# SwiGLU in Strassen's 2x2 blocks with gate/up and down as two stages, and a one-pass output projection

## The chip, the cores and the metric

The kernel runs on 1 core of one Trainium2 chip. The time is the device time of one execution in microseconds (us); lower is better. The engines are TensorE (PE, with its weight loads as PEld), VectorE (DVE), ScalarE (ACT), GpSimd (POOL) and SyncE (SP), whose queue issues the DMAs here. SBUF and PSUM are the memories on the core (matmuls write PSUM); a DRAM tile lies outside the core.

## The reference

Two layers on x of 1024 rows (S) by 1024 columns (D), all in float32; layer 0 mixes tokens by sliding-window attention (A), layer 1 by stick-breaking attention (B), and each is followed by a SwiGLU of width 2816:

```python
def swiglu(h, w_gate, w_up, w_down):
    return (jax.nn.silu(h @ w_gate) * (h @ w_up)) @ w_down

cond = jax.nn.silu(c)
for i in range(2):
    mod = (cond @ ada_w[i] + ada_b[i])[:, None, :]
    sh1, sc1, g1, sh2, sc2, g2 = jnp.split(mod, 6, axis=-1)
    h = rmsnorm(x, norm1_g[i]) * (1.0 + sc1) + sh1
    y = attention_A_or_B(h)            # ends with o @ w_o
    x = x + g1 * y
    h = rmsnorm(x, norm2_g[i]) * (1.0 + sc2) + sh2
    x = x + g2 * swiglu(h, w_gate[i], w_up[i], w_down[i])
```

## The kernel before

Every float32 product is made of three matmuls (`mm3`): each operand is split into a high part, which ScalarE casts to float32r, and a low part, which VectorE gets by subtracting the high from the whole (`split_w`, `sub`); the matmuls are high x high, high x low, low x high, each 128 rows by 128 columns of stationary weights with 512 moving columns. A weight tile `wr` of 128x1024 is loaded by SP, split into `wh` and `wl`, and used.

After the attention of a layer has written its heads' outputs to DRAM (`odA`, `odB`), `out_proj` multiplies them by the output weights in two passes of 512 columns (`c` = 0 and 1). For each of eight blocks of 128 rows it reloads the block (`or`), casts it on ScalarE (`oh`), subtracts on GpSimd (`ol`), and runs 24 matmuls; VectorE adds the result to x (`xt`), which stays in SBUF. The first pass is spread over the attention's end by the scheduler, which orders instructions by their dependences and the code. After blocks 0 to 3 and 4 to 7 of the second pass, `norm_half` normalizes the rows, turns them by TensorE and splits them (`hth`, `htl`).

`swiglu` then goes over 11 pairs of 128-column slices: for a pair it computes gate and up for both slices (banks `psd` and `psz`), Silu on ScalarE and the product on VectorE (`sg`), splits it (`hh`, `hl`), and, one pair behind, the down product of the pair before for all 16 blocks of output, which VectorE adds from PSUM (`pst`, `psa`) to `xt`:

```python
        for c in range(NC):
            hid = [gate_up(2 * c), gate_up(2 * c + 1)]
            ada_some(ada_per)
            ...
            if prev is not None:
                down(c - 1, prev, False)
            prev = hid
```

`ada_some` puts conditioning work between: each step loads a 128x1024 tile of `ada_w` (`ada`), and VectorE accumulates it (`acc`, L257). In layer 0 there are five a pair, in layer 1 none. The gate row of the conditioning (`grow`) multiplies the down weights on VectorE (L319). GpSimd has no work in `swiglu`. Layer 0's results go to DRAM tiles `xsp` for the second mixer, layer 1's to the output, block by block as the last pair ends.

## Time and profile before

| | |
|---|---|
| median of 3 runs | 2609.93 us (2608.35 to 2610.12) |
| span of the profiled execution | 2603.6 us |
| TensorE busy | 2508.4 us (96%), 11932 matmul records |
| VectorE busy | 1501.7 us (58%) |
| ScalarE busy | 930.9 us (36%) |
| GpSimd busy | 256.8 us (10%) |
| mean granted TensorE clock | 0.989 |

The span runs from the first to the last instruction of the execution that was profiled; the time of an execution also holds what lies around it, so the median is 6.3 us above the span. Busy time of an engine says how long it worked, not that something waited for it.

### The profile page before, as it was taken

What the parts mean: (1) busy time and instruction counts of PE and PEld (TensorE: products, weight loads), DVE (VectorE), ACT (ScalarE), POOL (GpSimd) and SP (SyncE); (2) the same over time, 40 slices, a digit from 0 to 9 for tenths busy, and PEclk for the clock granted to TensorE, in tenths of its full rate; (3) what the DMA queues carried; (4) which work ended last, traced back from release to release, by engine and by line L of the source; (5) the groups of instructions that cost most, each with busy time, mean ns of one, the idle gap of its engine ahead of it and who ended that gap; (6) DMA issues with size and microseconds to landing.
All of it is one profiled execution on the core that took longest, in us unless ns stands there. A gap on an engine that the chain in (4) does not pass through costs nothing.

```text
span 2603.6 us, 30732 instructions
## 1 busy us (share of the span) xinstructions
PE 2508.4 (96%) x11932; PEld 2021.0 (78%) x11932; DVE 1501.7 (58%) x2229; ACT 930.9 (36%) x1789; POOL 256.8 (10%) x385
## 2 busy tenths in 40 slices
PE   5799889999999999999999999999999999999999
PEld 5677677888888888777777777767788888888887
DVE  6689866535435445456777887786533333333334
ACT  4487733211111111135566666564421111111110
POOL 2445551000000000010000000003300000000000
PEclk9899999999999999999999999999999999999999
DMA  8113683413323323121110001134321111111101
GB/s 269 57 36 102 184 204 92 122 57 105 92 71 105 89 74 102 51 97 34 33 32 25 25 23 32 31 110 109 78 65 49 49 49 49 49 49 49 49 17 65
DMA packets 199409, 194.03 MB, mean 75 GB/s; under 512 B 8144, under 2 KB 169056, under 8 KB 199264
## 3 DMA queue, kind: packets, MB, share of 16 engines
q1 hardware_dynamic: 198640, 191.92, 25.6%
q8 instruction: 94, 1.54, 0.2%
q14 instruction: 51, 0.42, 0.1%
q10 hardware_dynamic: 624, 0.14, 0.0%
HBM read 175.26 MB, written 16.78 MB: 74 GB/s over the span
## 4 chain that ended last, share of the span: by engine, by line
PE 77%; DVE 10%; ACT 5%; DMA 4%; POOL 3%; issue 3%; SPq 0%; ACTq 0%; POOLq 0%; DVEq 0%
PE psd L97 29%; PE psz L97 22%; PE pst L97 14%; PE psa L97 9%; PE pst L105 2%; DMA ada<-in_ada_w_dram 2%; DVE acc L257 1%; DVE wl L302 1%; DVE nb L818 1%; ACT sm L523 1%; DVE al L108 1%; ACT ah L835 1%; POOL ol L302 1%; DVE bb L820 1%; DMA wr<-in_w_down_dram 0%
## 5 line engine op out<-in xcount | busy, mean ns | idle before, releaser
L97 PE MATMUL psd<-hth,wh 128*128 128x512 f32 x1088 | 431.3, 396 | 1.1 <-ACT nt L345 1.1
L97 PE MATMUL psd<-hth,wl 128*128 128x512 f32 x1088 | 430.6, 396 | 0.0
L97 PE MATMUL psd<-htl,wh 128*128 128x512 f32 x1088 | 428.8, 394 | 0.0
L97 PE MATMUL psz<-htl,wh 128*128 128x512 f32 x704 | 274.3, 390 | 0.0
L97 PE MATMUL psz<-hth,wh 128*128 128x512 f32 x704 | 274.3, 390 | 0.0
L97 PE MATMUL psz<-hth,wl 128*128 128x512 f32 x704 | 274.0, 389 | 0.0
L302 DVE TENSOR_TENSOR wl<-wr,wh 128x1024 fp32r<-128x1024 f32 x122 | 152.5, 1251 | 181.8 <-ACT wh L301 180.3
L301 ACT CAST wh<-wr 128x1024 fp32r<-128x1024 f32 x122 | 128.5, 1056 | 349.2 <-PE psd L97 174.0
L97 PEld LDWEIGHTS psd<-hth,wh 128*128 128x128 f32 x1088 | 204.6, 188 | 45.0 <-issue 5.0
L97 PEld LDWEIGHTS psd<-hth,wl 128*128 128x128 f32 x1088 | 204.6, 188 | 41.8 <-issue 3.4
L685 DVE TENSOR_TENSOR xt<-pst,xt 128x512 f32<-128x512 f32 x242 | 165.2, 689 | 124.3 <-PE pst L97 124.2
L97 PEld LDWEIGHTS psd<-htl,wh 128*128 128x128 f32 x1088 | 204.7, 188 | 40.1 <-issue 2.3
L668 DVE TENSOR_TENSOR sg<-psz,sg 128x512 f32<-128x512 f32 x88 | 60.6, 688 | 276.0 <-PE psz L97 276.0
L97 PE MATMUL pst<-dh,hh 128*128 128x512 f32 x484 | 189.9, 393 | 2.8 <-DVE xt L685 2.3
L97 PE MATMUL pst<-dl,hh 128*128 128x512 f32 x484 | 189.6, 392 | 0.8 <-DVE dl L302 0.8
L97 PE MATMUL pst<-dh,hl 128*128 128x512 f32 x484 | 189.0, 391 | 0.0
L301 ACT CAST dh<-wr 128x1024 fp32r<-128x1024 f32 x44 | 44.9, 1052 | 387.3 <-PE pst L97 379.4
L818 DVE TENSOR_TENSOR_SCAN nb<-nb,ones 128x128 f32<-128x128 f32 (+7 forms) x128 | 169.5, 1342 | 4.4 <-ACT nb L813 4.3
L670 ACT CAST hh<-sg 128x512 fp32r<-128x512 f32 x88 | 54.6, 621 | 286.1 <-DVE sg L668 286.1
L97 PEld LDWEIGHTS psz<-hth,wl 128*128 128x128 f32 x704 | 132.2, 188 | 27.8 <-issue 0.2
L97 PEld LDWEIGHTS psz<-htl,wh 128*128 128x128 f32 x704 | 132.0, 187 | 27.8 <-issue 0.5
L97 PEld LDWEIGHTS psz<-hth,wh 128*128 128x128 f32 x704 | 132.2, 188 | 27.5 <-issue 0.2
(258 smaller groups left out, 4699.5 us busy)
## 6 DMA issues: line engine op xcount, KB each, us to landing
ada<-in_ada_w_dram SPq DMA_DIRECT2D x96, 512.0 KB, 4.4
wr<-in_w_gate_dram SPq DMA_DIRECT2D x44, 512.0 KB, 4.0
wr<-in_w_up_dram SPq DMA_DIRECT2D x44, 512.0 KB, 4.9
wr<-in_w_down_dram SPq DMA_DIRECT2D x44, 512.0 KB, 3.7
wr<-in_wqkv_b_dram SPq DMA_DIRECT2D x24, 512.0 KB, 3.9
or<-odA SPq DMA_DIRECT2D x32, 256.0 KB, 4.6
or<-odB SPq DMA_DIRECT2D x32, 256.0 KB, 4.5
wr<-in_wqkv_a_dram SPq DMA_DIRECT2D x10, 512.0 KB, 5.8
```

Of the source, the lines that this page charges most:

```text
L97: nc.tensor.matmul(o, l, r, start=start, stop=stop)
L105: nc.tensor.transpose(o, i, ident[:n, :n])
L108: return nc.vector.tensor_tensor(o, a, h.bitcast(F32), op=ALU.subtract)
L257: i = nc.vector.scalar_tensor_tensor(a, wt, condT[:, j : j + 1], a, op0=ALU.mult, op1=ALU.add)
L301: nc.scalar.copy(h, raw)
L302: (eng or nc.vector).tensor_tensor(l, raw, h.bitcast(F32), op=ALU.subtract)
L523: nc.scalar.activation(sm[:, h], sm[:, h], AF.Exp, bias=nm_[:, h : h + 1], scale=r[:, h : h + 1], accum_out=su[:, h : h + 1])
L668: nc.vector.tensor_tensor(sg, pu, sg, op=ALU.mult)
L670: nc.scalar.copy(hh[:, c0 : c0 + 512], sg)
L685: nc.vector.tensor_tensor(xs, pb, xs, op=ALU.add)
L818: nc.vector.tensor_tensor_scan(rv, rv, ones[:, 0:1].to_broadcast([P, L]), initial=1.0, op0=ALU.mult, op1=ALU.mult)
L820: nc.vector.tensor_tensor(bb[:, 0 : L - 1], bb[:, 0 : L - 1], nb[:, 1:L], op=ALU.mult)
```

## The change

*Output projection.* `out_proj` now loads the whole rows of the output weights, splits them, and runs both column halves of a block together, so each block is loaded and split once instead of twice. The sums go to `xsp` in DRAM as well. The norm keeps the same steps, but its results are the four quarters of the turned activations: B11 and B21 from rows 0 to 511 (columns 0 to 511 and 512 to 1023 of D), B12 and B22 from the other rows. VectorE makes from them T1 = B12 - B11, T2 = B22 - T1, T3 = B22 - B12 and N4 = B21 - T2, and seven operands (B11, B21, T1, T2, T3, N4, B22) are split and kept.

*SwiGLU.* The products are made by Strassen's scheme (the form of Winograd), seven products of blocks for eight. `gates` goes over 11 chunks of 256 columns: GpSimd forms four sums of each weight's quarters, each operand is split (`sh`, `sl`, six tiles each), and each of seven products of each weight is 12 matmuls; VectorE adds PSUM results to the first product `p1`. The gate values of a chunk are written to a DRAM tile `hid`. Only when all chunks are done, `down` starts: the accumulators `xa` are loaded from `xsp`, and pairs of `hid` and down weights in three rounds of 4, 4 and 3 chunks. In each round GpSimd forms eight sums per chunk and adds 12 results to the accumulators, VectorE multiplies the weights by the gate row and splits, and TensorE runs 7 products of 12 matmuls per chunk. `ada_some` uses the three buffers `wr` of the new pool `wf` in layer 0.

```diff
+    def out_proj(wo, od, x_src, x_dst, row, side_h, side_w, l, gi):
...
+        wcur[:] = [wf, "wr", 3]
...
+        def block(b):
+            raw = op.tile([P, KT, P], F32, tag="or", name=nm("or"), bufs=1)
+            for par in range(2):
+                nc.sync.dma_start(raw[par * HD : (par + 1) * HD], od(b, par))
+            oh, ol = split_w(raw, [P, KT, P], op, "oh", "ol", bufs=2, eng=nc.gpsimd)
...
+            for c in range(2):
+                cs_ = slice(c * 512, c * 512 + 512)
+                pb = bank_any()
+                for k in range(KT):
+                    wh, wl = W[k // 2]
+                    mm3(pb, oh[:, k], ol[:, k], wh[:, k % 2, cs_], wl[:, k % 2, cs_], k == 0, k == KT - 1)
+                nc.vector.tensor_tensor(xt[:, cs_], pb, xt[:, cs_], op=ALU.add)
+            nc.sync.dma_start(x_dst[b], xt)
...
+        def put(n, kk, t):
+            h, l_ = H[n]
+            nc.scalar.copy(h[:, kk], t)
+            sub(l_[:, kk], t, h[:, kk])
...
         for b in range(NB):
-            block(b, 0, W, lambda: bank("d"))
+            block(b)
             ada_some(1)
+            if b == 3:
...
+                rows(range(4))
+                for k in range(KT):
+                    put("B11" if k < 4 else "B21", k % 4, col(range(4), k))
...
+        rows(range(4, 8))
+        for kk in range(4):
+            b12 = col(range(4, 8), kk)
+            b22 = col(range(4, 8), kk + 4)
+            t1 = np_.tile([P, 512], F32, tag="nt", name=nm("nt"), bufs=4)
+            h11, l11 = H["B11"]
+            h21, l21 = H["B21"]
+            tt(t1, b12, h11[:, kk].bitcast(F32), op=ALU.subtract)
+            tt(t1, t1, l11[:, kk].bitcast(F32), op=ALU.subtract)
+            tt(b12, b22, b12, op=ALU.subtract)
+            put("B22", kk, b22)
+            tt(b22, b22, t1, op=ALU.subtract)
+            put("T2", kk, b22)
+            put("T3", kk, b12)
+            put("T1", kk, t1)
+            tt(t1, h21[:, kk].bitcast(F32), b22, op=ALU.subtract)
+            tt(t1, t1, l21[:, kk].bitcast(F32), op=ALU.add)
+            put("N4", kk, t1)
...
+    def split_s(wf, src, shape):
+        h = wf.tile([P, 512], F32R, tag="sh", name=nm("sh"), bufs=6)
+        l = wf.tile([P, 512], F32R, tag="sl", name=nm("sl"), bufs=6)
...
+        nc.scalar.copy(hv, src)
+        nc.vector.tensor_tensor(lv, src, hv.bitcast(F32), op=ALU.subtract)
+        return h, l
...
+        def chunk(c):
+            m = []
+            for w in (w_gate[l], w_up[l]):
+                raw = wf.tile([P, KT, 2 * P], F32, tag="wr", name=nm("wr"), bufs=3)
...
+            for x in m:
+                A = x["A"]
+                pt_(A[1, 0], A[1, 0], A[1, 1], op=ALU.add)
+                pt_(A[0, 0], A[1, 0], A[0, 0], op=ALU.subtract)
+                pt_(A[0, 1], A[0, 1], A[0, 0], op=ALU.subtract)
+                x["Y"] = bank("z")
+                mms(x, x["Y"], A[0, 0], "T2", True)
+                x["u2"] = tile_()
+                tt(x["u2"], x["Y"], x["p1"], op=ALU.add)
...
+            for x in m:
+                mms(x, x["Z"], x["A"][0, 1], "B22", False)
+                tt(x["u2"], x["Z"], x["u2"], op=ALU.add)
+            for n, i, j in (("p1", 1, 0), ("u3", 1, 1), ("u2", 0, 1)):
+                g = m[0][n]
+                nc.scalar.activation(g, g, AF.Silu)
+                tt(g, m[1][n], g, op=ALU.mult)
+                nc.sync.dma_start(hid[c][:, i, j * 512 : j * 512 + 512], g)
...
+    ROUNDS = (4, 4, 3)
...
+                for nm_, src in (("A", hid[c]), ("B", w_down[l][2 * c * P : 2 * (c + 1) * P].rearrange("(k p) n -> p k n", p=P))):
...
+                    nc.sync.dma_start(raw, src)
+                    if nm_ == "B":
+                        tt(raw, raw, row[:, None, :].to_broadcast([P, 2, D]), op=ALU.mult)
...
+            def prod(banks, a, b, start, before=None):
+                for j, x in enumerate(pairs):
+                    if before:
+                        before(x)
+                    ah, al = split_s(wf, a(x), [P, 512])
+                    bh, bl = split_s(wf, b(x), [P, 512])
+                    for t in range(4):
+                        s_ = slice(t * P, (t + 1) * P)
+                        mm3(banks[t], ah[:, s_], al[:, s_], bh, bl, start and j == 0, j == n - 1, not start)
...
+                pt_(xacc[t + 4][:, lo], xacc[t + 4][:, lo], p, op=ALU.add)
...
+            def s1(x):
+                pt_(x["tA"], x["A"][:, 0, hi], x["A"][:, 1, hi], op=ALU.add)
+                pt_(x["tB"], x["B"][:, 0, hi], x["B"][:, 0, lo], op=ALU.subtract)
...
+            def s4(x):
+                pt_(x["A"][:, 0, lo], x["A"][:, 0, lo], x["A"][:, 0, hi], op=ALU.subtract)
+                pt_(x["B"][:, 0, hi], x["B"][:, 1, hi], x["B"][:, 0, hi], op=ALU.subtract)
+
+            prod(X, lambda x: x["A"][:, 0, lo], lambda x: x["B"][:, 0, hi], False, s4)
+            for t in range(4):
+                u = p2.tile([P, 512], F32, tag="u", name=nm("u"), bufs=3)
+                tt(u, X[t], p1[t], op=ALU.add)
+                pt_(xacc[t + 4][:, hi], xacc[t + 4][:, hi], u, op=ALU.add)
```

Four places of the new order of instructions, each engine's own. TensorE at the end of layer 0's attention, before (VA and DV are the attention's values, `KTs` its keys, `qs` its queries; `oh` and `ol` the projection's block, `wh` and `wl` its weights):

```order
L97 MATMUL psd_3828<-wh_3801,ol_3823 128x512
L97 MATMUL psa_3463<-ph_3459,VA 128x512
L97 MATMUL psz_3428<-KTs,QT_3392 128x256 x4
L97 MATMUL psd_3828<-wh_3808,oh_3822 128x512
L97 MATMUL psa_3463<-pl_3460,VA 128x512
L97 MATMUL psa_3463<-ow_3466,DV 128x512
L493 MATMUL pst_3559<-identr,qs_3552 128x128
L97 MATMUL psa_3463<-ow_3469,DV 128x512
```

and now:

```order
L97 MATMUL psa_3762<-ph_3758,VA 128x512
L97 MATMUL psa_3762<-pl_3759,VA 128x512
L97 MATMUL psa_3762<-ow_3765,DV 128x512
L97 MATMUL psa_3762<-ow_3768,DV 128x512
L97 MATMUL psd_3858<-Wh_816_3820,oh_3852 128x512
L97 MATMUL psd_3858<-Wl_817_3821,oh_3852 128x512
L97 MATMUL psd_3858<-Wh_816_3820,ol_3853 128x512
```

The projection's matmuls stood among the attention's; now the first one stands behind the last of the attention.

VectorE at the end of layer 0's norm, before (the casts and subtractions of the last three slices):

```order
L108 TENSOR_TENSOR htl_949_4543<-nt_4609,hth_948_4542 128x512
L346 CAST hth_948_4542<-nt_4618 128x512
L108 TENSOR_TENSOR htl_949_4543<-nt_4618,hth_948_4542 128x512
L346 CAST hth_948_4542<-nt_4627 128x512
L108 TENSOR_TENSOR htl_949_4543<-nt_4627,hth_948_4542 128x512
L346 CAST hth_948_4542<-nt_4636 128x512
```

and now (`nt` are the turned slices and the sums made of them, `hB`, `hT` and `hN` the casts, `lB`, `lT` and `lN` the low parts; `sl` the low parts of weights; the end of the last of four such pairs of slices and the rows behind it):

```order
L108 TENSOR_TENSOR lN_920_4489<-nt_4594,hN_919_4488 128x512
L679 TENSOR_TENSOR nt_4625<-nt_4625,lB_828_3846 128x512
L680 TENSOR_TENSOR nt_4616<-nt_4623,nt_4616 128x512
L682 TENSOR_TENSOR nt_4623<-nt_4623,nt_4625 128x512
L108 TENSOR_TENSOR lT_922_4491<-nt_4625,hT_921_4490 128x512
L108 TENSOR_TENSOR lT_918_4487<-nt_4616,hT_917_4486 128x512
L108 TENSOR_TENSOR lT_916_4485<-nt_4623,hT_915_4484 128x512
L686 TENSOR_TENSOR nt_4625<-hB_829_3847,nt_4623 128x512
L687 TENSOR_TENSOR nt_4625<-nt_4625,lB_830_3848 128x512
L108 TENSOR_TENSOR lN_920_4489<-nt_4625,hN_919_4488 128x512
L703 TENSOR_TENSOR sl_4734<-wr_4647,sh_4733 128x512
L703 TENSOR_TENSOR sl_4756<-wr_4650,sh_4755 128x512
```

Where a cast and a subtraction stood for each slice, there are 11 operations for each pair of slices, and the third product's weights (`sl_4734` and `sl_4756`, of T2) follow after the last of them.

VectorE at the step from chunk 3 to chunk 4 of layer 0's gates, now (`f` are gate values, `acc` the conditioning's accumulation; there is no such place before):

```order
L257 TENSOR_SCALAR acc_5832<-ada_5830,condT 128x1024
L279 SCALAR_TENSOR_TENSOR gscT<-adaT,cols 128x8
L260 SCALAR_TENSOR_TENSOR acc_5832<-ada_5834,condT,acc_5832 128x1024
L764 TENSOR_TENSOR f_5664<-pst_5754,f_5664 128x512
L260 SCALAR_TENSOR_TENSOR acc_5832<-ada_5837,condT,acc_5832 128x1024
L768 TENSOR_TENSOR f_5642<-f_5664,f_5642 128x512
L260 SCALAR_TENSOR_TENSOR acc_5832<-ada_5840,condT,acc_5832 128x1024
L703 TENSOR_TENSOR sl_5851<-wr_5843,sh_5850 128x512
```

The first split of chunk 4's gate weight, `sl_5851`, stands behind the last additions of chunk 3 (`f_5664`, `f_5642`) and three accumulations.

SP at the end of layer 0's gates. Before, it issued here the last down weights and the first of the second mixer:

```order
L317 DMA wr_8904<-in_w_down_dram 128x1024
L317 DMA wr_8911<-in_w_down_dram 128x1024
L251 DMA ada_9046<-in_ada_w_dram 128x1024
L317 DMA wr_9063<-in_w_down_dram 128x1024
L317 DMA wr_9070<-in_w_down_dram 128x1024
L312 DMA wr_9437<-in_wqkv_b_dram 128x8x128
```

and now (`hid` are writes of gate values, `xa` accumulators, `rx` a pair's two halves):

```order
L769 DMA hid_3786<-f_7659 128x512
L769 DMA hid_3786<-f_7777 128x512
L888 DMA xa_7951<-xsp_3787 128x1024
L769 DMA hid_3786<-f_7737 128x512
L888 DMA xa_7953<-xsp_3788 128x1024
L888 DMA xa_7955<-xsp_3789 128x1024
L888 DMA xa_7957<-xsp_3790 128x1024
L888 DMA xa_7959<-xsp_3791 128x1024
L888 DMA xa_7961<-xsp_3792 128x1024
L888 DMA xa_7963<-xsp_3793 128x1024
L888 DMA xa_7965<-xsp_3794 128x1024
L795 DMA rx_7974<-hid_3777 128x2048
```

Between the last two writes of gate values and the pairs' loads, the loads of seven accumulators were put; the other pairs' loads follow `rx_7974`.

## Rows read from the trace of the kernel before

**Rows 1.** the page: span, busy time, chain by engine
```profile
span 2603.6 us, 30732 instructions
...
PE 2508.4 (96%) x11932; PEld 2021.0 (78%) x11932; DVE 1501.7 (58%) x2229; ACT 930.9 (36%) x1789; POOL 256.8 (10%) x385
...
PE 77%; DVE 10%; ACT 5%; DMA 4%; POOL 3%; issue 3%; SPq 0%; ACTq 0%; POOLq 0%; DVEq 0%
...
```

**Rows 2.** the chain that ended last, 478 to 490: start, us, what
```profile
...
480.69 5.44 PE psd L97 x24
...
```

**Rows 3.** windows: length, busy us of PE, PEld, DVE, ACT, POOL, PEclk, DMA, GB/s
```profile
...
290.00:337.00 47.00, 44.08 (x223) 34.45 (x222) 40.74 (x83) 30.20 (x80) 25.78 (x21) 1.00 0.77 224
...
357.00:425.00 68.00, 59.94 (x282) 49.73 (x281) 42.83 (x52) 29.69 (x41) 28.37 (x24) 0.95 0.59 146
425.00:1090.00 665.00, 661.39 (x2950) 546.37 (x2949) 315.43 (x383) 116.33 (x150) 0.00 (x0) 1.00 0.29 88
...
1828.00:1878.00 50.00, 46.06 (x233) 38.43 (x232) 22.00 (x34) 21.85 (x32) 21.51 (x22) 1.00 0.37 74
1878.00:2603.00 725.00, 720.45 (x3171) 594.50 (x3170) 286.62 (x364) 122.75 (x160) 0.00 (x0) 1.00 0.16 48
...
```

**Rows 4.** windows of the tile oh's matmuls, 280 to 340 and 1740 to 1790
```profile
...
sum 60.00, PE 26.42; mean PE 4.40
...
sum 50.00, PE 12.15; mean PE 2.43
```

**Rows 5.** the page, DMA issues: count, KB each, median us to landing
```profile
...
or<-odA SPq DMA_DIRECT2D x32, 256.0 KB, 4.6
...
```

**Rows 6.** groups by line and form: count, busy us, mean ns, idle before
```profile
...
L257 DVE SCALAR_TENSOR_TENSOR acc<-ada,condT,acc 128x1024 f32<-128x1024 f32 x77 | 101.2, 1315 | 76.6 <-DMA ada<-in_ada_w_dram 76.3
...
L302 POOL TENSOR_TENSOR ol<-or,oh 128x1024 fp32r<-128x1024 f32 x32 | 81.7, 2553 | 104.3 <-ACT oh L301 95.7 <-PE psd L97 7.8 <-DMA xt<-in_x_dram 0.8
...
L301 ACT CAST oh<-or 128x1024 fp32r<-128x1024 f32 x32 | 33.6, 1051 | 48.0 <-PE psd L97 35.9 <-PE pst L97 3.3 <-PE psz L97 3.3
...
L484 POOL TENSOR_TENSOR qs<-qn,qs 128x512 fp32r<-128x512 f32 x16 | 21.6, 1356 | 13.2 <-ACT qs L483 13.2
...
```

**Rows 7.** the timeline of VectorE and of TensorE, 415 to 422
```profile
...
415.49 0.68 DVE L622 TENSOR_TENSOR xt<-psa,xt 128x512 f32<-128x512 f32 x1
...
420.92 0.69 DVE L108 TENSOR_TENSOR htl<-nt,hth 128x512 fp32r<-128x512 f32 x1
421.52 0.42 DVE L346 CAST hth<-nt 128x512 fp32r<-128x512 f32 x1
...
419.22 0.33 PE L105 MATMUL psd<-ident,xn 128*128 128x128 f32 x1 [0.96 <-DVE xn L336]
...
```

**Rows 8.** windows of 5 and 20 us near loads
```profile
...
15.00:20.00 5.00, 4.14 (x20) 3.71 (x19) 4.21 (x5) 2.52 (x4) 1.57 (x3) 1.00 1.02 413
20.00:25.00 5.00, 0.00 (x0) 0.00 (x0) 4.86 (x5) 0.00 (x0) 0.00 (x0) 0.73 1.09 338
380.00:400.00 20.00, 15.80 (x75) 13.61 (x74) 13.40 (x19) 8.85 (x13) 6.68 (x7) 0.83 0.79 221
...
```

**Rows 9.** the timeline of GpSimd and of VectorE, 342 to 352
```profile
...
342.80 2.39 POOL L302 TENSOR_TENSOR ol<-or,oh 128x1024 fp32r<-128x1024 f32 x1 [6.64 <-ACT oh L301]
349.51 3.08 POOL L302 TENSOR_TENSOR ol<-or,oh 128x1024 fp32r<-128x1024 f32 x1 [4.33 <-ACT oh L301]
...
343.60 3.80 DVE L597 TENSOR_TENSOR wr<-wr,grow 128x1024 f32<-128x1024 f32 x2 [1.05 <-DMA wr<-in_wo_a_dram]
...
349.13 1.22 DVE L302 TENSOR_TENSOR xl<-wr,xh 128x1024 fp32r<-128x1024 f32 x1
```

**Rows 10.** the timeline of GpSimd and of VectorE, 308 to 312
```profile
...
308.84 2.39 POOL L302 TENSOR_TENSOR ol<-or,oh 128x1024 fp32r<-128x1024 f32 x1 [0.81 <-DMA xt<-in_x_dram]
...
310.26 0.67 DVE L108 TENSOR_TENSOR pl<-pst,ph 128x512 fp32r<-128x512 f32 x1
...
```

**Rows 11.** the timeline of SP's queue, its first loads
```profile
...
7.90 10.42 SPq L251 DMA_DIRECT2D ada<-in_ada_w_dram  x6
...
```

More of the change, by code (lines that the diff above doesn't have):

```diff
@@ new lines, in block, with rows @@
+            nc.sync.dma_start(x_dst[b], xt)
+            xts[b] = xt
+        def rows(bs):
+            for b in bs:
+                junk = np_.tile([P, D], BF16, tag="junk", name=nm("junk"), bufs=1)
+                ss = cons.tile([P, 1], F32, tag="ss", name=nm("ss"), bufs=3)
+                nc.scalar.activation(junk, xts[b], AF.Square, scale=1.0 / 32.0, accum_out=ss)
+                nc.gpsimd.tensor_scalar(ss, ss, EPS, None, op0=ALU.add)
+                nc.gpsimd.tensor_tensor(ss, ss, mhalf[:, 0:1], op=ALU.pow)
+                nc.vector.tensor_scalar(xts[b], xts[b], ss, None, op0=ALU.mult)
@@ new lines, in out_proj @@
+            if b == 3:
+                if l == 0:
+                    while ada_list:
+                        ada_some(1)
+                    gsc_make(0, 1)
+                rows(range(4))
+                for k in range(KT):
+                    put("B11" if k < 4 else "B21", k % 4, col(range(4), k))
+        pools.close(cm_o)
+        pools.close(cm_W)
+        cm_h2, h2 = pools.open(nm("h2"), side_w)
+        for n in ("T2", "T3", "N4", "T1", "B22"):
+            H[n] = (h2.tile(Q4, F32R, name=nm("h" + n)), h2.tile(Q4, F32R, name=nm("l" + n)))
@@ new lines, in mixer @@
+    def mixer(l, wo, od, x_src, row, side_h, side_w, gi, ada_per, rest, finish):
+        H, wf, cm_f, cm_h1, cm_h2 = out_proj(wo, od, x_src, xsp, row, side_h, side_w, l, gi)
+        if l == 0:
+            ada_list.extend(ada_late)
+        cm_fp, fp = pools.open(nm("fp"), side_h)
+        row2 = gates(l, H, wf, fp, hid, ada_per)
+        rest()
+        pools.close(cm_fp)
+        pools.close(cm_h1)
+        pools.close(cm_h2)
+        cm_xa, xa = pools.open(nm("xa"), "right")
+        cm_p2, p2 = pools.open(nm("p2"), "left")
+        xacc = []
+        for b in range(NB):
+            t = xa.tile([P, D], F32, name=nm("xa"))
+            nc.sync.dma_start(t, xsp[b])
+            xacc.append(t)
+        down(l, wf, p2, xacc, hid, row2, lambda bs: finish(xacc, bs))
+        pools.close(cm_p2)
+        pools.close(cm_f)
+        return xacc, cm_xa
```

302 lines of the change are left out of this document (164 added, 138 removed).

## The prediction

> **What bounds the kernel now.** I read the page first: TensorE is busy 96% of a span of 2603.6 us, it takes 77% of the chain that ended last, and GpSimd 10%, VectorE 58% [rows 1]. The chain in the middle of a channel mixer is TensorE alone, and 24 matmuls of 512 columns take 5.44 us there: 0.2267 us each [rows 2]. The table of windows shows where TensorE is not full [rows 3]: the two mixers' long stretches are 99% busy (425 to 1090, 1878 to 2603), while output projection and norm (290 to 337 and 357 to 425 in layer 0, 1828 to 1878 in layer 1) leave 11 and 4 us idle. So a matmul less is worth 0.2267 us, as long as the other engines keep up. They have much room now: VectorE is busy 315 us of the 665 in 425 to 1090, GpSimd for nothing.
>
> **What goes.** Per layer, gate and up are 22 slices x 2 weights x 2 halves x 8 blocks x 3 = 2112 matmuls, down 22 x 8 x 2 x 3 = 1056. Seven eighths of both is 2772 of 3168, so 396 fewer, 89.8 us a layer, **179.5 us in all** (6.9% of the span). The splits of down's values (a cast and a subtraction per slice) go too, but lay beside TensorE.
>
> **What comes, in order of time.**
>
> *Output projection.* Before, its first column half ran inside the attention's tail. TensorE was busy 26.4 us by 340 in layer 0, and 12.2 by 1790 in layer 1, with matmuls that read the tile `oh` [rows 4]; these are two of every three, but a record reaches into the next matmul, so this is about the time of all three. Now all of it starts after the last attention block (the rows of TensorE's order). The other engines' share there was 40.7 of 47 us on VectorE [rows 3], so the attention can hardly get shorter without it: lost 24 (20 to 26.4) and 12 (8 to 12.2). Then TensorE waits for the first block: the `or` loads are queued on SP behind the last attention write and two weight loads, land after 4.6 us [rows 5], are cast (1.05) and subtracted on GpSimd (2.55) [rows 6]: 8.2, and with the write and issues 12 (8 to 14) per layer. The transposes of the first four blocks stand ahead of block 4 in TensorE's order and wait for the row chain: 3.7 us from the last add to the first transpose now [rows 7], 5 (2 to 7) per layer. Sum 41 and 29. The old idle time of these stretches, 11 and 4 [rows 3], is replaced by it: 30 and 25.
>
> *The combined activations.* T1, T2, T3, N4 and B22 are made by 11 VectorE operations on two SBUF operands for each of four slices, 44 in a row, and the split of the third product's weights stands behind them (VectorE's order). Subtractions of 128x512 last 0.69 and let the next start after 0.60 [rows 7]: 26 to 30 us. GpSimd's sums of the first weights contend with them for SBUF (below). Under it lie 48 matmuls of the first two products (10.9) and some 4 us of transposes. Exposed: 13 without GpSimd, 20 with its six sums of 1.2; I take 18 (11 to 28) per layer, with a last row chain of 4: 22.
>
> *Gates.* In steady state a chunk is 168 matmuls, 38.1 us. VectorE's 17 two-operand operations of 0.60 and GpSimd's 8 of 1.2 sum to 20, so it stays TensorE's. In layer 0, however, five conditioning loads per chunk share three buffers with the two weights, and at four boundaries of ten the split of the next chunk's weight is put behind the last product's sums (VectorE's order: the first `sl` of chunk 4 behind L764, L768 and three accumulations of 1.3 [rows 6]). TensorE has then nothing queued: two of these at 10 and two at 5, 30 us (0 if the weights come in time, 45 if all ten show). Layer 1 has no such loads: 0.
>
> *Start of down.* SP issues in order: the last gate value, then seven accumulators from DRAM (3.7 MB), then the pairs of 2 MB (SP's order). At the 338 to 413 GB/s that the loads reached [rows 8], pair 1 is there 16 us after the write at the best and 25 with it, each other pair 5 to 6 us later, so the first product of four pairs ends some 40 us after the last gate instead of 10.9. Layer 1 differs in order a little: 29 and 18, less 10 each for work that VectorE and GpSimd do ahead meanwhile: 19 and 8 (0 to 29).
>
> *Down itself.* This is the largest term, and it rests on who may read SBUF. GpSimd's subtraction of 128x1024 at 342.80 took 2.39 us. VectorE's two multiplications of two SBUF operands, due at 343.60, took 3.80 for 2.4 of work: exactly what was left of GpSimd's, and then theirs. The opposite happens at 349.51, where GpSimd needed 3.08 behind VectorE's 1.22 [rows 9]. VectorE with a PSUM operand is not held: at 310.26 it took 0.67 inside GpSimd's 2.39 [rows 10]. Half of 2.39 is 1.2 for 128x512 (the shape itself, in the rotary step, had a mean of 1.36 [rows 6]). A round of four pairs has 56 subtractions on VectorE (0.60: 33.6), 4 multiplications of 128x2048 by the gate row (twice the 1.22 of an operation of 1024 [rows 9] less overlap, 2.35: 9.4), and 44 operations on GpSimd (8 a pair and 12 additions to the accumulators, 1.195 each: 52.6): 95.6 us, for 336 matmuls of 76.2. Three rounds (4, 4, 3 pairs) come to 266 if the two engines exclude each other and never wait otherwise, against 924 matmuls of 209.5. They also wait for unevenness: the second product of a round is TensorE's (10.9 against 9.6), the sixth is not (19.2), and only six split tiles stand ahead. I take 58 a layer (0 to 99.5: no exclusion, or 309 in sum, if VectorE's 24 PSUM additions a round, 0.60 each, come on top of all three rounds).
>
> The rows show it for 1024 columns at chance meetings; whether it holds when both engines have a queue of 512-column operations, no row shows. The Trainium skill ("SBUF — State Buffer", section "SBUF: two separate sides") says that GpSimd and VectorE share one pair of ports as an exclusive lock: whichever starts first has it for the whole instruction, against VectorE's operations with two SBUF inputs. By that rule down would be the 266 or more whatever the lengths, and 209.5 if the rows were a matter of long shapes; the trace agrees with the rule at 3.80 for 2.4 and 3.08 for 2.39.
>
> *Rest.* The last four accumulators leave in a row after the last product, while now they leave block by block; six loads were issued in 10.42 us [rows 11], so three issues more are 5. The step from layer 0 to layer 1 costs the same within 3. TensorE's granted clock is 1.00 in the long stretches [rows 3], but 0.73 in five microseconds in which it did nothing, and 0.83 in twenty with gaps of 4 in sum [rows 8], part of them at 1.2 instead of 2.4 GHz; the new idle stretches cost some 10 in all (0 to 20).
>
> **Sum.** Layer 0: 30 + 22 + 30 + 19 + 58 - 89.8 = +69. Layer 1: 25 + 22 + 0 + 8 + 58 - 89.8 = +23. Rest 18. The profiled span becomes 2603.6 + 110 = 2714; the median of the runs is 6.3 above the span: **2720 us**, 4% more.
>
> **Rivals.**
> 1. *No exclusion (the faster side).* If operations of 512 columns of the two engines pass each other, down is TensorE's and 2 x 58 us go: 2604. It decides at the price of the exclusion: 58 us a layer make this forecast, 3 make no change (2610), below 3 the kernel is faster; without the 30 us at layer 0's chunk boundaries, which hang on the same VectorE queue, 2574. For it: either engine alone has 33.6 + 9.4 or 52.6 us of work for 76 of TensorE's. Against: both rows of [rows 9]. Chance 0.17, of which 0.13 faster.
> 2. *The stages start full.* The loads of the first block, of the chunks and of the pairs come in time: 24 + 30 + 27 go, and 2639 is left, slower still. For it: 88 and 48 GB/s in the long stretches leave the queues room [rows 3]. Against: what must be loaded at a start stands behind values written just before, and the queues gave 338 to 413 GB/s where pressed [rows 8]. 0.10.
> 3. *Worse.* VectorE's PSUM additions come on top in every round (309 for down) and the starts cost their upper ends: 2720 + 2 x 41.5 + 15 = 2818. For it: GpSimd holds sums of the next round, which wait for loads, ahead of this round's. 0.15.
> 4. The forecast, 2670 to 2770: 0.58.
>
> The range leaves out about a tenth at either end: 2590 to 2810. A measurement of this kernel tells 0.2% (5 us) from no change. Faster by more: 0.14 (0.13 of rival 1, the rest of rival 2); within: 0.04; slower: 0.82.
>
> **What would show it.** TensorE's records fall from 11932 by some 790. In down, TensorE's busy share is near 75 to 80%, GpSimd busy over half, and VectorE's 128x512 subtractions with two SBUF operands last well over 0.69 on the mean while those with PSUM do not. TensorE has a gap of some 12 us between the last attention matmul and the first of the projection, one of 20 before the third product of chunk 0, and one of 20 to 30 where down starts. The prediction is wrong if down's TensorE share is above 92%, or if those gaps are not there.

## The result, and the profile after

The changed kernel takes **2790.27 us** (median of 4 runs, 2782.01 to 2791.39) against 2609.92 of the kernel before: 1.0688 times as long, 95% interval 1.0672 to 1.0703. The forecast was 2720 in a range of 2590 to 2810, slower with a chance of 0.82. The direction and the mechanisms held; the loss is 180 us where 110 were summed.

The lines of the page that answer to [rows 1] (the PEclk line has TensorE's granted clock in 40 slices, in tenths):

```profile
span 2780.3 us, 31321 instructions
...
PE 2434.1 (88%) x11140; PEld 1915.7 (69%) x11140; DVE 1950.5 (70%) x2643; ACT 1149.4 (41%) x2281; POOL 874.2 (31%) x793
...
PEclk9999688999999979999999999997979999999999
...
PE 55%; DVE 21%; POOL 8%; DMA 7%; ACT 5%; issue 4%; SPq 0%; ACTq 0%; DVEq 0%; POOLq 0%
...
```

TensorE has 792 matmul records fewer (11932 before), as forecast, but is busy only 74 us less (its mean granted clock is 0.942 instead of 0.989), and its share falls from 96% to 88%; VectorE and GpSimd took over its part of the chain (21% and 8%, 10% and 3% before). The same windows as in [rows 3], cut at the stages of the new kernel: attention's tail, projection and norm, combined activations, gates, down, in both layers (busy us and counts of PE, PEld, DVE, ACT, POOL; then PEclk, DMA share and GB/s):

```profile
...
291.00:337.00 46.00, 26.36 (x96) 18.78 (x96) 42.88 (x67) 26.72 (x62) 17.72 (x16) 0.68 0.46 137
337.00:461.00 124.00, 102.16 (x466) 84.17 (x465) 33.86 (x46) 30.55 (x47) 29.18 (x27) 0.90 0.51 150
461.00:495.00 34.00, 10.05 (x24) 7.14 (x24) 33.07 (x44) 17.27 (x28) 9.45 (x6) 0.60 0.00 0
495.00:991.00 496.00, 448.97 (x1938) 360.28 (x1939) 312.26 (x374) 129.70 (x221) 131.17 (x83) 0.97 0.38 123
991.00:1286.00 295.00, 236.77 (x929) 180.29 (x928) 250.33 (x235) 96.92 (x173) 196.51 (x127) 0.91 0.24 92
1917.00:2035.00 118.00, 98.84 (x448) 81.36 (x448) 33.95 (x41) 31.39 (x47) 28.24 (x27) 0.91 0.46 134
2035.00:2069.00 34.00, 9.97 (x25) 7.04 (x24) 32.95 (x44) 17.27 (x29) 9.65 (x7) 0.60 0.00 0
2069.00:2486.00 417.00, 415.89 (x1824) 343.25 (x1825) 235.73 (x307) 133.43 (x221) 121.16 (x83) 1.00 0.27 91
2486.00:2774.00 288.00, 237.55 (x930) 182.33 (x928) 250.69 (x236) 92.01 (x164) 192.02 (x121) 0.92 0.21 82
...
```

The two stretches of down begin with a wait; from its end on, the windows are:

```profile
...
1014.00:1286.00 272.00, 233.29 (x913) 177.77 (x914) 245.53 (x231) 96.05 (x172) 195.03 (x126) 0.94 0.19 72
2501.00:2774.00 273.00, 233.56 (x912) 179.35 (x912) 245.88 (x232) 91.23 (x163) 190.63 (x120) 0.93 0.18 72
...
```

The kernel before has these windows from the attention's end to the first matmul of the SwiGLU, and for the SwiGLU, in both layers:

```profile
...
338.00:420.00 82.00, 73.61 (x349) 61.43 (x349) 53.98 (x57) 33.34 (x43) 33.91 (x26) 0.96 0.69 171
420.00:1161.00 741.00, 736.73 (x3287) 608.07 (x3286) 352.23 (x436) 136.70 (x177) 3.15 (x8) 1.00 0.29 87
1789.00:1877.00 88.00, 84.23 (x402) 70.17 (x401) 41.88 (x48) 36.91 (x47) 39.21 (x29) 1.00 0.56 115
1877.00:2599.00 722.00, 720.88 (x3174) 595.05 (x3173) 286.43 (x364) 123.75 (x161) 0.00 (x0) 1.00 0.15 48
...
```

So layer 0 took 82 + 741 us and now takes 124 + 34 + 496 + 295; layer 1 took 88 + 722 and now takes 118 + 34 + 417 + 288. Of the new kernel's stages only one shows TensorE full at full clock: layer 1's gates, 417 us for 1824 matmuls of 0.2267 (413.5).

In layer 0's down, after its start (groups by line and form; behind the first bar the busy time in us and the mean of one in ns):

```profile
...
L703 DVE TENSOR_TENSOR sl<-rx,sh 128x512 fp32r<-128x512 f32 x99 | 124.9, 1310 | 22.0 <-ACT sh L702 21.8
...
L797 DVE TENSOR_TENSOR rx<-rx,grow 128x2048 f32<-128x2048 f32 x9 | 24.9, 2762 | 0.0
...
L820 POOL TENSOR_TENSOR xa<-xa,p 128x512 f32<-128x512 f32 x12 | 21.8, 1847 | 0.8 <-ACT p L819 0.8
...
L833 DVE TENSOR_TENSOR xa<-psz,xa 128x512 f32<-128x512 f32 x6 | 3.7, 675 | 0.0
...
```

VectorE's subtractions with two SBUF operands take 1310 ns, nearly twice the 690 of [rows 7] (the 44 that read `tA` and `tB` take 1181 and 1026); its additions from PSUM (L833) take 675. GpSimd's additions on L820 take 1847, the other groups of its sums 1423 to 1825, all sums in the window 1.6 us on the mean; the shortest take 1.27 to 1.29. That is the exclusion of [rows 9], now all through a stage.

### The profile page after: what moved, and what is told of

The parts are those of the page before. It is cut to its first block, busy times and chain, and to the rows that moved or that the text cites. A ratio compares the mean times of both kernels' runs of the same rounds, so it can differ in the third digit from the quotient of the medians.

```text
span 2780.3 us, 31321 instructions
## 1 busy us (share of the span) xinstructions
PE 2434.1 (88%) x11140; PEld 1915.7 (69%) x11140; DVE 1950.5 (70%) x2643; ACT 1149.4 (41%) x2281; POOL 874.2 (31%) x793
## 4 chain that ended last, share of the span: by engine, by line
PE 55%; DVE 21%; POOL 8%; DMA 7%; ACT 5%; issue 4%; SPq 0%; ACTq 0%; DVEq 0%; POOLq 0%
PE psd L97 19%; PE psz L97 19%; PE pst L97 10%; DVE sl L703 7%; PE psa L97 4%; DMA ada<-in_ada_w_dram 3%; PE pst L105 2%; DVE rx L797 2%; DVE acc L260 2%; DMA wr<-in_w_up_dram 1%; POOL tA L836 1%; POOL rx L837 1%; ACT sh L702 1%; POOL tB L844 1%; POOL rx L856 1%
## 5 line engine op out<-in xcount | busy, mean ns | idle before, releaser
L702 ACT CAST sh<-wr 128x512 fp32r<-128x512 f32 x284 | 173.4, 621 | 473.5 <-PE psz L97 219.6
L703 DVE TENSOR_TENSOR sl<-wr,sh 128x512 fp32r<-128x512 f32 x284 | 259.6, 923 | 78.6 <-ACT sh L702 78.5
L703 DVE TENSOR_TENSOR sl<-rx,sh 128x512 fp32r<-128x512 f32 x200 | 252.3, 1309 | 67.4 <-ACT sh L702 67.0
L97 PE MATMUL psd<-hB,sh 128*128 128x512 f32 x352 | 145.5, 413 | 70.4 <-ACT f L735 35.9
L97 PE MATMUL psd<-hth,wh 128*128 128x512 f32 x384 | 157.3, 410 | 0.8 <-DVE Q L108 0.8
L97 PE MATMUL psd<-hth,wl 128*128 128x512 f32 x384 | 157.2, 409 | 0.0
L97 PE MATMUL psd<-htl,wh 128*128 128x512 f32 x384 | 155.4, 405 | 0.1
L97 PE MATMUL psd<-hB,sl 128*128 128x512 f32 x352 | 143.5, 408 | 0.7 <-DVE sl L703 0.7
L97 PE MATMUL psd<-lB,sh 128*128 128x512 f32 x352 | 143.3, 407 | 0.0
L97 PE MATMUL psz<-hT,sh 128*128 128x512 f32 x352 | 138.1, 392 | 5.1 <-DVE f L750 5.1
```

The costliest lines, as they stand in the source:

```text
L97: nc.tensor.matmul(o, l, r, start=start, stop=stop, skip_group_check=more)
L702: nc.scalar.copy(hv, src)
L703: nc.vector.tensor_tensor(lv, src, hv.bitcast(F32), op=ALU.subtract)
```

## Experiments

Spans of profiled executions are compared below where the difference is small: 2780.3 us for the changed kernel, whose time was 2782.01 in that run. Layer 0's gates vary by some 10 us from one kernel to the next though nothing there was changed (the time from the second product to the end of the first wait of down is 519 us in the changed kernel and 520 to 528 in four others), so a change of that size in a total means nothing; the waits themselves are read. The runs with one edit were timed once each.

**Down's sums on VectorE.** In `down`:

```diff
-        pt_ = nc.gpsimd.tensor_tensor
+        pt_ = nc.vector.tensor_tensor
```

> In down, the 44 sums and additions of a four-pair round go from GpSimd to VectorE, in both layers. If the two engines exclude each other from SBUF (my theory), VectorE alone needs 33.6 for splits, 9.4 for the gate row, 26.4 for the sums and 14.4 for PSUM additions, 84 us a round instead of some 98 measured, so down's 272 us become about 235 in each layer and the kernel about 2715 us; the low-part subtractions fall from a mean of 1.31 us to 0.69. If VectorE's own queue is what limits down and GpSimd relieves it (rival), 26.4 us more a round make down up to 340 us and the kernel 2860 or more.

Measured: 2711.92 us, 78 less. VectorE, the busier engine, got all the work of the less busy one, and the stage became shorter; its subtractions are back at 689 ns:

```profile
...
L703 DVE TENSOR_TENSOR sl<-rx,sh 128x512 fp32r<-128x512 f32 x200 | 128.4, 689 | 0.9 <-ACT sh L702 0.5
...
```
```profile
...
1027.00:1262.00 235.00, 220.59 (x945) 176.74 (x945) 231.69 (x358) 100.39 (x178) 5.40 (x12) 0.98 0.24 92
2475.00:2705.00 230.00, 215.41 (x912) 171.89 (x912) 227.32 (x352) 91.22 (x163) 0.00 (x0) 0.98 0.22 87
...
```

The windows from the first wait to the end of down were 272 and 273 us and are 235 and 230, with VectorE busy 99% of them. The theory's 235 is met. VectorE's own queue was not what limited the stage; the sum of what two engines hold SBUF for was.

**Down without the sums.** All calls of `pt_` in `down` are left out (a product takes a quarter as it is, `xa` gets a copy of the last two results), the matmuls stay:

```diff
...
-                pt_(x["tA"], x["A"][:, 0, hi], x["A"][:, 1, hi], op=ALU.add)
...
-            prod(Y, lambda x: x["tA"], lambda x: x["tB"], True, s1)
+            prod(Y, lambda x: x["A"][:, 0, hi], lambda x: x["B"][:, 0, hi], True)
```

> Leaves out all of GpSimd's sums in down and its additions to the accumulators (a product takes unsummed quarters in their place, and ScalarE copies the eight results per round that were added), so TensorE's matmuls, the splits and the loads stay. By my theory down is then TensorE's: 209.5 us of matmuls and little more, 215 instead of 272 after its start in each layer, the kernel about 2676 us, and TensorE's clock is back at 1.00 there. If the few split tiles ahead or the lower clock hold it (rival), it stays at 250 or more.

Measured: 2670.5 us, and the stage is TensorE's, within 12 us of its 209.5:

```profile
...
1020.00:1241.00 221.00, 216.73 (x950) 177.50 (x950) 166.15 (x244) 115.37 (x207) 7.67 (x15) 0.98 0.25 98
2448.00:2668.00 220.00, 211.53 (x912) 172.74 (x912) 159.39 (x232) 104.61 (x187) 0.00 (x0) 0.98 0.25 98
...
```

GpSimd's sums cost 51 and 53 us a layer after the start of down. The lookahead of six split tiles is enough, and the clock, 0.94 and 0.93 in the changed kernel's windows there, is 0.98 once TensorE is fed: what the lower clock took from down was a consequence of the waits.

**Buffers of their own for the conditioning.** After the projection of layer 0:

```diff
-            return fp.tile([P, 512], F32, tag="f", name=nm("f"), bufs=15)
+            return fp.tile([P, 512], F32, tag="f", name=nm("f"), bufs=11)
...
+        if l == 0:
+            wcur[:] = [fp, "ad", 2]
         row2 = gates(l, H, wf, fp, hid, ada_per)
         rest()
+        wcur[:] = [wf, "wr", 3]
```

> In layer 0's gates the conditioning loads get two buffers of their own, so the three of the weights hold weights alone; the gate tiles go from 15 to 11 to make room. If the shared buffers delay the next chunk's weight loads (my theory), the waits of up to 8.9 us at the chunks' borders go and layer 0's gates, 496 us, take 445 to 455, the kernel about 2745. If the order on VectorE is the cause (rival), the waits stay and the time is within 10 us of 2790. Layer 1 has no such loads: its 417 us show whether 11 gate tiles cost anything.

Measured: 2740.45 us, span 2738.7. Layer 0's gates take 454 us instead of 496, and no wait above 3 us is left at a chunk's border. Layer 1, which has no such loads, took 426 us from the second product to the last matmul before down's wait, 6 more than in the changed kernel; the version with five edits below has the 11 gate tiles too and took 420, so the fewer tiles need not cost anything. Layer 0's gates:

```profile
...
496.00:950.00 454.00, 440.66 (x1940) 358.41 (x1941) 310.70 (x379) 133.15 (x221) 126.05 (x83) 0.98 0.44 140
...
```

In the changed kernel the longest of the waits at a border looked like this, on TensorE, ScalarE, VectorE and SP:

```profile
...
671.25 0.79 PE L97 MATMUL psd<-hB,sh 128*128 128x512 f32 x1 [8.86 <-ACT sh L702]
...
```
```profile
...
670.57 0.62 ACT L702 CAST sh<-wr 128x512 fp32r<-128x512 f32 x1 [11.54 <-DMA wr<-in_w_gate_dram]
...
```
```profile
...
671.23 1.20 DVE L703 TENSOR_TENSOR sl<-wr,sh 128x512 fp32r<-128x512 f32 x1 [4.07 <-ACT sh L702]
...
```
```profile
...
661.88 0.33 SPq L254 DMA_DIRECT2D ada<-in_ada_w_dram  x1
663.20 0.38 SPq L718 DMA_DIRECT2D wr<-in_w_gate_dram  x1
...
```

TensorE waits 8.86 us for a cast, ScalarE 11.54 us for the weight, and SP could issue its load (663.20) only after a conditioning load, because the buffers go round: the weight's buffer is free when that of the conditioning tile three turns earlier is, and that one waited for the end of the chunk: VectorE's accumulation of a conditioning tile, among the chunk's last sums, ended at 663.17, and SP issued at 663.20. VectorE itself then waited 4.07 us for the cast, so its order alone did not hold the split up. It had a part through the shared buffers, and this run does not take it out: in the new program the next chunk's first split also stands ahead of the chunk's last gate value (L768) on VectorE.

**Accumulators behind the pairs.** The eight loads of `xa` move from `mixer` into `down`, behind the first round's pairs:

```diff
+            if r == 0:
+                for b in range(NB):
+                    nc.sync.dma_start(xacc[(b + 4) % NB], xsp[(b + 4) % NB])
...
-            t = xa.tile([P, D], F32, name=nm("xa"))
-            nc.sync.dma_start(t, xsp[b])
-            xacc.append(t)
+            xacc.append(xa.tile([P, D], F32, name=nm("xa")))
```

> The loads of the eight accumulators are issued behind the first four pairs instead of ahead of them. If the 3.7 MB ahead set when the first pair arrives (my theory), the wait of 19.9 us in layer 0 becomes about 10, in layer 1 that of 11.5 about 5, and the kernel is 10 to 18 us faster, 2775. If the last gate value's write and the freed buffers set it (rival), the waits stay within 3 us and so does the time.

Measured: 2784.11 us; the wait in layer 0 fell from 19.94 to 14.20 us, in between the two theories, that in layer 1 did not fall (11.52 and 12.84), and the total cannot be told from the changed kernel's. The changed kernel and then this run, layer 0 and layer 1 of each:

```profile
...
1014.42 0.79 PE L97 MATMUL psd<-sh,sh 128*128 128x512 f32 x1 [19.94 <-ACT sh L702]
2501.51 0.80 PE L97 MATMUL psd<-sh,sh 128*128 128x512 f32 x1 [11.52 <-ACT sh L702]
...
```
```profile
...
1019.28 0.79 PE L97 MATMUL psd<-sh,sh 128*128 128x512 f32 x1 [14.20 <-ACT sh L702]
2505.24 0.80 PE L97 MATMUL psd<-sh,sh 128*128 128x512 f32 x1 [12.84 <-ACT sh L702]
...
```

The order on SP was some 6 us of layer 0's wait (three of the eight accumulators still went ahead of the pairs). In layer 1 of the changed kernel it was nothing: there the accumulators' loads were issued from 2454.66 on, long ahead of the first pair's (2489.56). What remains there is that pair's own load, cast at 2495.98, and VectorE's multiplication by the gate row, for which the next cast waited 4.24 us.

**The gates' sums on VectorE.** The same line as in down, in `gates`:

> The eight sums of a chunk in gates go from GpSimd to VectorE, in both layers. If GpSimd's sums of chunk 0 hold the first six operations of the combined activations (1.7 us each instead of 0.68), these fall to 0.68 and the two waits there (7.0 and 17.2 us in layer 0) lose some 3 to 6 us in each layer; layer 1's gates stay at 417 us, TensorE's, since VectorE has 88 x 0.6 = 53 us more on 236 of 417; layer 0's 496 change by less than 15; in all 2790 becomes 2765 to 2785. If VectorE's order is what makes the gates late (rival), layer 0's gates grow by 30 or more.

Measured: 2750.76 us, span 2749.0, more than I expected. In the changed kernel VectorE's first six operations of the combined activations lay beside GpSimd's sums:

```profile
...
460.94 1.67 DVE L678 TENSOR_TENSOR nt<-nt,hB 128x512 f32<-128x512 f32 x1 [1.24 <-ACT nt L646]
...
469.25 1.74 DVE L682 TENSOR_TENSOR nt<-nt,nt 128x512 f32<-128x512 f32 x1
470.92 0.68 DVE L108 TENSOR_TENSOR lT<-nt,hT 128x512 fp32r<-128x512 f32 x1
...
```
```profile
...
457.89 2.94 POOL L733 TENSOR_TENSOR s<-wr 128x512 f32<-128x512 f32 x2
460.79 2.96 POOL L744 TENSOR_TENSOR wr<-wr 128x512 f32<-128x512 f32 x2
...
467.07 3.37 POOL L746 TENSOR_TENSOR wr<-wr 128x512 f32<-128x512 f32 x2
...
```

1.65 to 1.77 us each until GpSimd ends at 470.4, 0.68 from then on. With the sums on VectorE they start at full pace:

```profile
...
461.49 0.69 DVE L678 TENSOR_TENSOR nt<-nt,hB 128x512 f32<-128x512 f32 x1 [1.23 <-ACT nt L646]
...
```

That gave 6 us, and layer 0's gates another 17 (479 us); in layer 1 the stage before the gates gained 7 and the gates, TensorE's, did not change within 2. GpSimd's help there had only cost time.

**First projection loads ahead.** The loads of chunk 0's weights are issued behind the first `or` loads:

```diff
+                with (tc.issue_after(or0[0].ins) if c == 0 else ExitStack()):
+                    nc.sync.dma_start(raw, w[:, c * 2 * P : (c + 1) * 2 * P].rearrange("(k p) n -> p k n", p=P))
```

> The first chunk's gate and up weights (2 MB) are issued behind the first block's two loads of the projection instead of ahead of them. If what is queued ahead on SP makes the projection start late (my theory), TensorE's wait between attention and projection falls from 12.7 and 14.3 us to 8 or 9, and the kernel is 8 to 10 us faster. If the chain from the attention's last write through the landing, the cast and GpSimd's subtraction makes it (rival), the waits stay within 2 us.

Measured: 2782.73 us, span 2781.0. The waits fell as expected, from 12.71 and 14.31 us to 8.34 and 9.19, but layer 0's gates were 7 us slower in this run, and the total shows nothing. In the changed kernel, and then in this run:

```profile
...
336.06 1.05 PE L97 MATMUL psa<-ow,DV 128*128 128x512 f32 x2
349.82 0.80 PE L97 MATMUL psd<-Wh,oh 128*128 128x512 f32 x1 [12.71 <-ACT oh L304]
...
```
```profile
...
348.82 0.79 PE L97 MATMUL psd<-Wh,oh 128*128 128x512 f32 x1 [8.34 <-ACT oh L304]
...
```

**Five edits together.** Down's and the gates' sums on VectorE, the conditioning's own buffers, the accumulators behind the pairs, and the projection's first loads ahead:

> All of it together: down's and the gates' sums on VectorE, own buffers for the conditioning loads, accumulators behind the first pairs, first projection loads ahead. The single gains are 78, 50 and 6 us as measured, and 5 to 25 and 0 to 10 as expected of the two others: if they add, 2630 to 2655, still behind the kernel before by 1 to 2%. If the gains overlap (a wait that goes lets the next show), 2670 or more.

Measured: 2629.21 us (2622.76 to 2631.36), 1.0072 times the kernel before (1.0052 to 1.0091). The five runs' gains sum to 181 us from the medians and to 140 from the spans; together they give 161 and 152. So they add as far as single runs can tell, but not stage by stage: layer 0's gates fell from 496 to 454 with own buffers and to 479 with the sums on VectorE, and to 449 with both. Once the buffers are apart, GpSimd's sums cost some 5 us there and not 17:

```profile
...
483.00:932.00 449.00, 438.52 (x1942) 356.47 (x1943) 317.00 (x468) 133.23 (x221) 0.00 (x0) 0.99 0.44 140
...
```

**The first two products early.** Chunk 0's first two products are put ahead of the second norm half in the program, with a tile for the copies. To make room the gate tiles fall from 15 to 13, and the turned slices go through other PSUM banks; two lines of the edit:

```diff
...
+        m0 = first_two(l, H, wf, px)
         rows(range(4, 8))
...
```

> Chunk 0's first two products are put ahead of the second norm half in the program, with a tile of their own for the first product's copies, so those copies stand ahead of the casts of T1, T2, T3 and N4 on ScalarE (gate tiles 13 instead of 15 for room). If the second product waits only because the copy of the first stands behind these casts (my theory), the wait of 17.2 us splits: both products run before and under the combined activations, the third starts 5 to 7 us earlier, and the kernel is 10 to 14 us faster, 2777. If TensorE would wait for VectorE's 44 operations all the same and gains nothing by it (rival), 2785 to 2795.

Measured: 2794.93 us: no gain, as the rival said. The copies did move ahead of the casts, and the second product ran early, but TensorE ran both products ahead of the transposes, so the chain on VectorE began later (467.55 instead of 460.94, of which 2.3 us were there when the projection began) and the third product had to wait for its end all the same. The second product in the changed kernel, and then the third and VectorE's chain in this run:

```profile
...
495.20 0.79 PE L97 MATMUL psd<-hB,sh 128*128 128x512 f32 x1 [17.19 <-ACT f L735]
...
```
```profile
...
506.06 0.80 PE L103 MATMUL psz<-hT,sh 128*128 128x512 f32 x1 [36.30 <-ACT sh L710]
...
```
```profile
...
467.55 0.69 DVE L686 TENSOR_TENSOR nt<-nt,hB 128x512 f32<-128x512 f32 x1 [7.93 <-ACT nt L652]
...
503.62 0.69 DVE L114 TENSOR_TENSOR lN<-nt,hN 128x512 fp32r<-128x512 f32 x1 [0.68 <-ACT hN L657]
```

The third product started at 506.06 instead of 502.45, 1.4 us later when counted from the projection's start. The wait of 17.19 us in front of the second product was ScalarE's order, but moving the copy only moved the wait to the third product, which needs VectorE's 44 operations. An order with the transposes first and the second product under the chain was not run, so whether such an order would gain the 5 to 7 us stays open.

> The version with all five edits, with this sixth one (and one buffer instead of two for the conditioning loads): if the 10 to 14 us add to 2629, 2615 to 2620, 0.2 to 0.5% behind the kernel before. If VectorE, which now also has the gates' sums at that place, takes the gain, 2625 to 2632.

Measured: 2637.59 us, 1.0115 times the kernel before (1.0097 to 1.0132): 8 us worse than without that edit; the run alone was 5 us above the changed kernel's median. The one buffer less is not the reason: from the third product to the end of down's first wait layer 0 took 458 us, and 459 in the version with five edits.

**The overlap of projection and attention, alone.** In the kernel *before*, the first pass's loads are issued behind the attention's last write:

```diff
+            with (tc.issue_after(last_od[0].ins) if c == 0 else ExitStack()):
+                for par in range(2):
+                    nc.sync.dma_start(raw[par * HD : (par + 1) * HD], od(b, par))
```

> The kernel before, with one thing changed: the projection's first-pass loads are issued behind the attention's last write, in both layers, so nothing of the projection lies in the attention's tail. If the lost overlap and the late start cost what I took (24 + 12 in layer 0, 12 + 12 in layer 1, less idle time that they replace), the kernel goes from 2608 to 2650 or 2665, while the attention ends at the same time. If the attention gets shorter without the projection's work in it, or the overlap was worth nothing (rival), it stays below 2625.

Measured: 2668.99 us, 62.6 more than the kernel before on the same chip. The attention's last output comes at 338.8 us, as before (338.5), though TensorE is now idle for more than a third of its tail and its clock falls to 0.75 there; the projection then waits 8.96 us to start:

```profile
...
291.00:338.00 47.00, 29.02 (x117) 22.47 (x116) 37.26 (x71) 21.03 (x61) 13.45 (x16) 0.75 0.50 159
...
```
```profile
...
346.58 0.80 PE L98 MATMUL psd<-wh,oh 128*128 128x512 f32 x1 [8.96 <-ACT oh L302]
...
```

Layer 0's SwiGLU started 38 us later than in the kernel before; layer 1 lost the rest, 2 of it up to its attention's last output. So nearly all of that work had been free, beside a VectorE that was busy 40.7 of 47 us [rows 3], and the rearranged projection of the change gave it away: the 62.6 us, late starts among them, stand against the 71 by which projection and norm became longer.

**Block tiles placed low.** With the five edits, the tiles of a projection block (`op`) lie directly above the weights' buffers, the norm's tiles on the other side of SBUF, and layer 0's two sides are swapped:

```diff
+        cm_o, op = pools.open(nm("op"), side_w)
         cm_W, wpool = pools.open(nm("W"), side_w)
...
-        cm_o, op = pools.open(nm("op"), side_h)
...
-        x2d, row_a, "left", "right", 1, 5, rest0, fin0)
+        x2d, row_a, "right", "left", 1, 5, rest0, fin0)
```

> The version with five edits, and the projection's block tiles placed in SBUF right above the weights' buffers (the norm's tiles on the other side), where the memory is free before the attention ends, so the first blocks' loads can be issued between the attention's last writes, two blocks in layer 1, one just ahead of the last write in layer 0. The lost overlap was 38 and 24 us in the kernel before; if the place of these tiles made the projection late, I expect 4 of it back in layer 0 and 10 to 15 in layer 1: 2629 becomes 2610 to 2616, the kernel before's time. If the late start is the attention's own end (rival), 2625 or more.

Measured: 2603.43 us (10 runs), 0.9985 times the kernel before (0.9975 to 0.9994). TensorE waits 6.61 us in layer 0 and 2.26 in layer 1 before the first projection matmul, for the cast of the output weights now:

```profile
...
338.98 0.79 PE L97 MATMUL psd<-Wh,oh 128*128 128x512 f32 x1 [6.61 <-ACT Wh L304]
...
```
```profile
...
1799.06 0.50 PE L97 MATMUL psd<-Wh,oh 128*128 128x512 f32 x1 [2.26 <-ACT Wh L304]
...
```

With the tiles placed low, SP issues the first block's loads ahead of the attention's last write in layer 0:

```profile
...
330.81 1.27 SPq L619 DMA_DIRECT2D or<-odA  x2
333.73 0.48 SPq L557 DMA_DIRECT2D odA<-ob  x1
...
```

In the version with five edits they were issued at 342.63, behind it; in layer 1 the first of them now goes out at 1747.1, 50 us ahead of the attention's last output (1797.2), and went out at 1819.6, behind it (1818.6). So the place of these tiles had held the loads back. The whole kernel got 26 us shorter (29 by the spans), more than I had expected, but only 14 of the 29 lie where the placing acts: 6 up to the second product in layer 0, where the attention's last output also came 8 us earlier, and 8 at layer 1's projection. Another 11 lie in layer 0's gates and the start of down, and 4 in down and the second attention; these are not explained, and of the size by which layer 0's gates vary.

**First products summed once.** Besides, in `down` the first product of every round is added to one tile, and that to three quarters in the last round:

```diff
-                nc.scalar.copy(p, X[t])
-                pt_(xacc[t + 4][:, lo], xacc[t + 4][:, lo], p, op=ALU.add)
+                    tt(p1[t], X[t], p1[t], op=ALU.add)
...
-                tt(u, X[t], p1[t], op=ALU.add)
-                pt_(xacc[t][:, hi], xacc[t][:, hi], u, op=ALU.add)
+                tt(xacc[t][:, hi], X[t], xacc[t][:, hi], op=ALU.add)
```

> The same, and in down the first products of all rounds are summed in a tile of their own and added to three quarters of the accumulators once instead of in each round: 24 additions on two SBUF operands and 12 fewer PSUM additions against them, 12 operations of 0.60 fewer a layer on VectorE. If down is VectorE's (235 us for 209.5 of matmuls), 5 to 7 us a layer go: 10 to 14 below the other version, 2597 to 2605, and the kernel is at or just below the one before. If TensorE's refill decides (rival), within 4 of it.

Measured: **2596.82 us** (2592.54 to 2601.17, 6 runs), 0.9961 times the kernel before (0.9949 to 0.9974). It is 7 us below the last, half of what I expected; what limited the other half was not looked into further. This version, seven products for eight with the sums on VectorE, takes 0.4% less than the kernel before and 7% less than the changed one.

## Why the prediction was right, and where its sum was off

The terms, each a span between the same two events before and after (us):

| term | forecast | measured | how |
|---|---|---|---|
| matmuls saved, per layer | -89.8 | -89.8 | 792 records fewer in all, at 0.2267 each |
| projection to first product, layer 0, 1 | 30, 25 | 41, 30 | 124 - 82 (41 before rounding), 118 - 88 |
| combined activations | 22, 22 | 29, 29 | 34 less 5.4 for the first product's 24 matmuls |
| gates beyond matmuls | 30, 0 | 59, 3 | 496 - 413.5 - 23, 417 - 413.5 |
| down beyond matmuls, start and body | 77, 66 | 85, 78 | 295 and 288 less 209.5 |
| rest | 18 | 2 | what is left of 176.7 |

(The 23 us are what layer 0's SwiGLU took beyond its 718 us of matmuls before, conditioning among it; layer 1 had 4.) The spans differ by 176.7, the terms of the forecast sum to 110; with 2790 the measured time lies near the upper end of the range.

- **What bounds, and what goes:** right. A matmul less is worth 0.2267 us only where TensorE is fed, and layer 1's gates show it.
- **Projection:** the mechanism was right and is shown alone by the kernel before with late loads. The step took 36 of the overlap and 24 of the starts, and came out 11 and 5 us too low; what it missed is the placing of the tiles in SBUF, which held the loads back (some 14 us with the other placing).
- **Combined activations:** right in kind, 7 us too low a layer. I let two products lie under the chain, with one wait of 20 us before the third product; only the first lies there, most of its matmuls 0.43 us apart, at the lower of the clock's two levels (the granted clock of the stretch is 0.60). The waits, 7.0 and 17.2 us, stand inside the first product and before the second, which needs a copy that stands behind the chain's casts on ScalarE. GpSimd's sums cost 6 of the 29.
- **Gates of layer 0: the step that failed in size.** It put down 30 us at four borders, where 59 were lost, and told two causes, the three shared buffers and VectorE's order. The run with own buffers takes away 42 us, and the rows at the border show the late load. GpSimd's sums, which the step called harmless ("it stays TensorE's"), cost 17 in layer 0 beside the shared buffers and some 5 without them; both causes together are 47 of the 59. In layer 1 the sums were harmless.
- **Start of down:** 23 and 15 us to the first wait's end, for 19 and 8. The order on SP, which I gave most weight, was some 6 of it in layer 0 and nothing in layer 1; VectorE's multiplication by the gate row, 4.2 us of the wait, was no term of the step.
- **Down:** 58 a layer forecast, some 63 measured after the start; GpSimd's sums cost 51 and 53 of it by the run without them. VectorE's subtraction took 1310 ns with GpSimd beside it and 689 without, its additions with a PSUM operand 675 and 686. The Trainium skill's rule of exclusive ports that the prediction cites ("SBUF — State Buffer", section "SBUF: two separate sides") agrees with these rows. The step's 1.195 us for a sum on GpSimd, half of a longer one, was low, since the shortest take 1.27 to 1.29; with 1.28 its three rounds come to 277 (my estimate), against 272 and 273 measured. Its word "exactly" for [rows 9] is too strong: both rows are 0.15 to 0.2 us shorter than a full exclusion would make them.
- **Clock:** its 10 us stood within the 18 of the rest, of which 2 are left. What the lower clock cost lies inside the stages: down's clock was 0.94 and 0.93, and 0.98 when it was fed.

Rival 1 is refuted by the two runs on down, rival 2 by the waits at each start, and rival 3 came near in time (2818) for another reason: not down, which took 272 where it had 309, but layer 0's gates above all. That the total lies between the forecast and rival 3 is thus the sum of several steps put too low, not of one.

What stays open: the 12 us of layer 0's gates that neither cause explains, whether the second product can lie under the chain behind the transposes, and whether the overlap of projection and attention can be had in full beside seven split operands in SBUF; only the two placings told here were run.

## What to carry to other kernels

Fewer matmuls pay only if what makes them fewer fits on the other engines: count, stage by stage, the time of all operations with two SBUF operands on VectorE *plus* those on GpSimd, and compare that sum with TensorE's. If it is larger, as in down (95.6 us a round by the prediction's sum, for 76.2 of matmuls), moving work from GpSimd to the busier VectorE can make the stage faster. A smaller sum is no guarantee: in layer 0's gates GpSimd's sums cost 17 us although the sum was below TensorE's time. A rearranged stage loses the overlap that the old one had with its neighbour, and where tiles lie in SBUF, or which loads share a ring of buffers, can decide when the next stage's loads may start.

## What I had not expected of the hardware

- Both engines pay for meeting: VectorE's 128x512 subtraction took 1310 ns on the mean for 689 alone, GpSimd's sums of the same shape 1.4 to 1.85 us by group, where the shortest took 1.27 to 1.29.
- An attention tail with TensorE a third less busy and at a clock of 0.75 had its last output at 338.8 us, as before (338.5); in the changed kernel the clock was 0.68 and the last output came at 337.8. Here the lower clock cost nothing, as TensorE was not what the tail waited for.
